# Two-layer decoder trunk: roots on ScalarE, relisted mixer steps, first loads issued together, last half stored in quarters

## The chip, the cores and the metric

The kernel runs on one core of a Trainium2 chip. The metric is the device time of one execution in microseconds (us); less is better. Engines are called as in the profile: PE is TensorE (PEld its weight loads), DVE is VectorE, ACT is ScalarE, POOL is GpSimd, SP is SyncE, which issues most of the DMAs.

## The reference

Two layers over x (256 tokens, 1024 features, float32), conditioned on a vector c. Cut to what matters:

```python
c_act = silu(c)
for l in range(2):
    sh1, sc1, gt1, sh2, sc2, gt2 = split(c_act @ w_ada[l] + b_ada[l], 6)
    h = rms_norm(x, g_pre_mix[l]) * (1 + sc1) + sh1
    q, k, v, pz = split(h @ w_in[l])              # 512 columns each
    ao = moba_attention(rotary(q), rotary(k), v)  # 8 heads, causal (one block of 256)
    po = multiscale_pool(pz, w_pool[l], pool_scale[l])
    y = concat(rms_norm(ao, a_gain[l]), rms_norm(po, p_gain[l])) @ w_out[l]
    x = x + gt1 * rms_norm(y, g_post_mix[l])
    h = rms_norm(x, g_pre_ffn[l]) * (1 + sc2) + sh2
    a, g = split(causal_conv3(h @ w_up[l]) + conv_b[l])   # 2816 columns each
    x = x + gt2 * rms_norm((silu(a) * g) @ w_down[l], g_post_ffn[l])
```

`rms_norm(x, g)` is `x / sqrt(mean(x*x) + 1e-6) * g`. Every norm thus needs a reciprocal root of one number per token.

## The kernel before

**Precision and parts.** Each float32 weight block is split on the chip into a high part (a cast on ScalarE, `Stream.high`, line 135) and a low part (a subtraction on VectorE, `Stream.low`, line 143), and each product is made as three matmuls (`mm3`, line 174). Activations are split in the same way. Weights thus pass through DMA, ScalarE and VectorE before TensorE can use them.

**Loads.** `Stream` (lines 77 to 159) holds one list of weight units in the order of use. `pump` (line 102) issues the next loads on SyncE's queue as long as one of 4 raw slots of 1 MB is free; a unit's slot is freed when its last part has been made or, for the modulation weights, when VectorE's reductions over them are done. Parts go into 8 high and 8 low buffers of 512 KB; in the FFN, parts are made up to `LEAD` = 6 ahead.

**Start** (lines 1000 to 1027, and `mixer`, line 475). c, x (two tiles of 128 tokens), the identity and the biases are loaded, all on SyncE's queue, then the first weight units. A matmul spreads c over the partitions, ScalarE applies Silu. VectorE squares and sums x, POOL takes the power -0.5, VectorE scales both tiles, TensorE transposes them (16 of 128 x 128), ScalarE copies the result in four pieces. Then the input projection of layer 0 runs over 8 chunks of 128 features: for each, `chunk(k)` (line 501) makes two reductions on VectorE (`dot`: modulation columns), the scale, two parts and the normalised activation; then 24 matmuls follow. The first modulation block and the first and last projection blocks are loaded as two half units, each of which takes a slot.

**Mixer steps** (`steps`, line 554). Everything between the input projection and the FFN is cut into some 250 small steps with two-letter names, and `ORDER[l]` (line 29) lists them by hand, one list per layer. While the list is worked off, the engines are "held" (`Kept`, line 59): each keeps its instructions in the order of the list, so an instruction that waits holds up all behind it on its engine. Names that matter here: `cq ck cv cz` copy the projections out of PSUM (a capital letter: on ScalarE instead of VectorE), `sc mx ex rc nm pt at` are the attention, `wo` the output projection, `gp gq` the gate products over a gate weight block, `gr gs gc gd gm gn` turn them into columns, `gt gg` make the gate row, `s2` reductions for the FFN's scale, `hi lo` make weight parts. The end of a list is a chain: `ss` (column sums of squares), `r1 r2` (roots of both group norms), `ad` (adds the two halves of y), `yq` (squares of y), `yG` (y times gate), `ry` (root), `xu` (x updated), `xs` (squares of x), `rx` (root), `xN` (x scaled), `tr` (transposes for the FFN). `tx` and `ts` load ScalarE's tables for Exp and for Silu by an activation of one dummy column (`table`, line 291).

**Roots.** `rstd` (line 386) takes two half sums, and on POOL adds epsilon, adds the second half, and raises to -0.5: three instructions. `r1 r2` (lines 774 to 784) use three instructions on VectorE and two on POOL.

**FFN** (`ffn`, line 885 on). For each of 22 column groups: up-projection, convolution (`conv_glu`: two scalings on ScalarE, four multiply-adds on VectorE, Silu on ScalarE between them), a split, down-projection. Six down-projections are kept for the end (`DEFER`), where `tail` (line 409) works on the four blocks of 128 tokens by 512 columns: matmuls, squares on ScalarE, product with the gate on VectorE; after both halves the root, the update of x, and either the norm for the next layer or the store. Outside the lists the compile-time scheduler is free to reorder.

## Time and profile before

| what | value |
|---|---|
| median of 3 runs | 610.45 us (610.43 to 611.44) |
| the profiled execution | 611.41 us |
| its span, first to last instruction | 609.6 us |
| TensorE busy / weight loads | 584.1 us (96%) / 504.0 us (83%) |
| VectorE / ScalarE / POOL busy | 490.4 (80%) / 376.7 (62%) / 29.8 us (5%) |
| mean granted clock of TensorE | 0.993 |
| DMA | 149.08 MB, mean 245 GB/s |

How to read it: the span is what the engines' records cover, the execution's time has a little more around it. TensorE is busy nearly all the time, so time can be won only where it stands or runs at less than its full rate. Nearly all instructions carry one line number, 69, because `Kept` records them there; they are told apart by tile names (`qk v pz`: input projection, `y yp`: output projection, `u d`: FFN, `T`: transposes, `hi lo`: weight parts, `hh hl`: activation parts, `sqs`: squares, `ra ry rx`: roots).

### The profile page before, as it was taken

The page shows a single profiled execution, that of the slowest core. Times are in us where ns is not written, and L with a number is a line of the kernel's source. Part 1 is how long each engine was busy: PE and PEld are TensorE (multiplying, and loading weights), DVE is VectorE, ACT ScalarE, POOL GpSimd, SP SyncE. Part 2 cuts the span into 40 slices and gives each one's busy share as a digit, 9 for nine tenths or more (in the row PEclk, how much of TensorE's full clock was granted, in tenths as well). Part 3 has the DMA queues.
Part 4 walks back from the last instruction along what each step waited for, and adds up shares of the span by engine and source line. Part 5 has one row for each costly group of instructions (what it writes and reads, how often), then busy time and mean ns, then how long its engine had stood idle before and what let it go on. Part 6 is the DMA issues. An engine that isn't in the chain of part 4 may idle for free.

```text
span 609.6 us, 9688 instructions
## 1 busy us (share of the span) xinstructions
PE 584.1 (96%) x3732; PEld 504.0 (83%) x3732; DVE 490.4 (80%) x865; ACT 376.7 (62%) x664; POOL 29.8 (5%) x62
## 2 busy tenths in 40 slices
PE   5999899699999999999999999979999999999995
PEld 3887567499999999999858876659999999999984
DVE  5998798789999998978559687688989787777753
ACT  4457786777656555557447688768765655656641
POOL 1000100400000000000010000140000000000001
PEclk9999999899999999999999999999999999999999
DMA  8999996667888867864339846765676566455001
GB/s 297 402 395 340 395 366 260 276 210 275 336 297 322 301 262 277 300 236 145 132 114 378 293 145 252 286 228 189 216 280 263 208 215 255 162 197 205 4 1 69
DMA packets 22768, 149.08 MB, mean 245 GB/s; under 512 B 2881, under 2 KB 3265, under 8 KB 6210
## 3 DMA queue, kind: packets, MB, share of 16 engines
q1 hardware_dynamic: 22722, 148.47, 66.0%
...
HBM read 147.41 MB, written 1.05 MB: 244 GB/s over the span
## 4 chain that ended last, share of the span: by engine, by line
PE 76%; DVE 10%; DMA 5%; ACT 4%; POOL 2%; issue 2%; POOLq 0%; DVEq 0%; SPq 0%; ACTq 0%
PE u L69 41%; PE d L69 20%; PE qk L69 3%; DVE lo L69 3%; PE y L69 2%; DVE raw L69 2%; DMA raw<-w_out_d 2%; PE pz L69 2%; PE v L69 2%; ACT hi L69 1%; DMA raw<-w_in_d 1%; DMA raw<-w_gt_d 1%; PE T L69 1%; POOL rx L69 1%; ACT sqs L69 1%
## 5 line engine op out<-in xcount | busy, mean ns | idle before, releaser
L69 DVE TENSOR_TENSOR lo<-raw,hi 128x1024 fp32r<-128x1024 f32 (+1 forms) x184 | 217.7, 1197 | 29.5 <-ACT hi L69 29.1
L69 ACT CAST hi<-raw 128x1024 fp32r<-128x1024 f32 (+1 forms) x184 | 185.8, 1030 | 58.1 <-DMA raw<-w_in_d 14.8
L69 PE MATMUL u<-hh,hi 128*128 128x256 f32 x704 | 182.2, 282 | 0.3 <-ACT h L69 0.2
L69 PE MATMUL u<-hh,lo 128*128 128x256 f32 x704 | 181.8, 281 | 0.0
L69 PE MATMUL u<-hl,hi 128*128 128x256 f32 x704 | 138.8, 282 | 0.5 <-DVE hl L69 0.5
L69 PEld LDWEIGHTS u<-hh,hi 128*128 128x128 f32 x704 | 132.5, 188 | 2.0 <-ACT hh L69 0.4
L69 PEld LDWEIGHTS u<-hh,lo 128*128 128x128 f32 x704 | 132.5, 188 | 1.4
L69 PEld LDWEIGHTS u<-hl,hi 128*128 128x128 f32 x704 | 107.1, 188 | 1.0 <-DVE hl L69 0.9
L69 DVE SCALAR_TENSOR_TENSOR cv<-u,vecs,cv 128x254 f32<-128x254 f32 (+1 forms) x176 | 83.1, 479 | 26.5 <-ACT cv L69 24.2
L69 ACT ACTIVATE cv<-u,vecs 128x256 f32<-128x256 f32 x88 | 48.7, 558 | 56.0 <-PE u L69 55.9
L69 DVE CUSTOM_DVE_ANT_0 raw<-raw,cbc,vecs 128x1024 f32<-128x1024 f32 x64 | 81.2, 1278 | 1.1 <-DMA raw<-w_g_d 0.9
L69 PE MATMUL d<-hi,sh 128*128 128x512 f32 x176 | 69.7, 396 | 0.0
L69 PE MATMUL d<-lo,sh 128*128 128x512 f32 x176 | 69.2, 393 | 0.0
L69 PE MATMUL d<-hi,sl 128*128 128x512 f32 x176 | 68.6, 394 | 0.0
L69 PEld LDWEIGHTS d<-hi,sl 128*128 128x128 f32 x176 | 33.0, 188 | 7.8 <-DVE sl L69 0.2
L69 PEld LDWEIGHTS d<-hi,sh 128*128 128x128 f32 x176 | 33.1, 188 | 6.6 <-ACT sh L69 0.3
L69 PEld LDWEIGHTS d<-lo,sh 128*128 128x128 f32 x176 | 33.2, 189 | 6.1
L69 ACT CAST sh<-cv 128x256 fp32r<-128x256 f32 x44 | 17.6, 404 | 33.3 <-DVE cv L69 33.3
L69 ACT ACTIVATE cv<-cv 128x256 f32<-128x256 f32 x44 | 18.4, 417 | 17.7 <-DVE cv L69 17.6
L69 ACT ACTIVATE sm<-sm,st 128x128 f32<-128x128 f32 (+1 forms) x52 | 22.0, 448 | 6.6 <-DVE st L69 6.5
L69 DVE TENSOR_TENSOR sl<-cv,sh 128x256 fp32r<-128x256 f32 x44 | 18.4, 421 | 9.1 <-ACT sh L69 9.1
L69 PE MATMUL qk<-hi,hh 128*128 128x512 f32 x64 | 23.0, 419 | 2.9 <-ACT hh L69 2.9
...
## 6 DMA issues: line engine op xcount, KB each, us to landing
...
```

Source lines behind the costliest of these rows:

```text
L69: r = op(*a, **k)
```

## The change

1. *Roots on ScalarE.* `rstd` becomes one addition on POOL (first half sum plus epsilon), one Sqrt on ScalarE with that as its bias and the second half sum as its input, one reciprocal on VectorE. In the lists `ry` and `rx` become three steps each (`ey sy ry`, `eX sx rx`). `r1 r2` become one Sqrt, a reciprocal and a product. `ts` now loads the table of Sqrt; the one of Silu is loaded in `ffn` after the norm, and that of Sqrt again behind its last Silu. The start's own root stays on POOL.
2. *Lists anew.* Both `ORDER` lists are written anew. `cK0` and `cZ1` move copies to ScalarE in layer 0, some `tQ` go back to VectorE; in layer 1 the gate steps (`gc gm gt gg`) move from the end of the list to before and among the attention's steps; in layer 0 they stay near the end.
3. *First loads at once, first chunk shared.* c, identity and biases are loaded on ScalarE's queue. The second modulation block and the second projection block are loaded, in halves, into part buffers (`home`) instead of raw slots, so that the first three blocks of each kind are issued without a wait. Blocks in halves now take one slot. The start up to chunk 1 is held in program order. The cast of the first part is shared by ScalarE and VectorE, the scaling of the second x tile moves to ScalarE, three of the four copies of x come after chunk 0, and TensorE makes 8 and then 12 transposes of the identity into a bank that is written later (`warm`).
4. *Last stores.* The last half of x is updated and stored in two quarters (of 256 columns).

The diff, cut to its core:

```diff
 ORDER = [
...
-    "ml3 ss ts gc r1 gm wo101 r2 wo201 gt0 ad10 gt1 gg0 ad11 wo210 gg1 ad00 wo310 ad01 wo300 yG10 hi8 wo301 "
-    "yG00 yq00 wo111 yG01 yq01 wo211 hi9 lo8 wo311 ry0 yq11 xu01 gq1 yq10 yG11 gq2 xs01 xu00 ry1 xs00 gq3 "
-    "xu11 xs11 xu10 rx0 lo9 xs10 gs xN00 xN01 gd rx1 tr00 xN10 gn tr01 xN11 tr10 hi10 tr11 hi11 lo10 lo11",
+    "sq3 wo200 sa3 ml3 ss gm r1 gt1 r2 wo201 gg1 ad00 gt0 ad01 gg0 wo300 ad10 wo301 yq00 yG00 ey0 wo210 yq01 "
+    "sy0 yG01 ry0 wo310 xu00 gq1 yq10 ey1 yG10 xs00 wo011 eX0 xu01 ad11 gq2 hi8 hi9 wo111 lo8 wo211 xs01 sx0 "
+    "wo311 lo9 yG11 yq11 gq3 sy1 rx0 ry1 xN00 gs xu11 gd xu10 tr00 hi10 gn lo10 xs10 eX1 xs11 sx1 xN01 rx1 "
+    "xN10 tr01 hi11 xN11 tr10 tr11 lo11",
...
-    "sa3 hi12 ss hi13 lo12 wo200 cy10 r1 cy11 wo001 wo101 lo13 r2 hi14 wo201 lo14 hi15 gc ad00 wo010 gm wo110 "
-    "ad11 gt1 wo300 ad01 gg1 ad10 wo301 yq00 wo210 lo15 yq01 gt0 gg0 wo111 ry0 wo211 yG00 xu00 wo311 yG01 "
-    "wo310 yq11 xu01 yq10 gq2 yG10 xs00 yG11 gq3 xs01 ry1 xu11 xs11 xu10 rx0 xN00 xs10 xN01 tr00 gs tr01 gd "
-    "rx1 xN10 xN11 gn tr10 tr11",
+    "sa2 ml2 sa3 hi12 yP12 hi13 lo12 yP13 hi14 lo13 hi15 ss r1 lo14 r2 wo200 cy10 cy11 wo201 lo15 wo010 ad01 "
+    "wo110 ad00 wo301 ad10 wo300 yq01 wo011 yq00 yG00 ey0 sy0 wo210 ad11 ry0 wo310 xu00 wo111 yq10 yG01 ey1 "
+    "wo211 xs00 xu01 eX0 wo311 yG10 yq11 yG11 gq2 sy1 ry1 xs01 sx0 gq3 xu10 xu11 rx0 xs10 eX1 xs11 xN00 xN01 "
+    "sx1 rx1 tr00 gs xN10 tr01 xN11 gd tr10 gn tr11",
 ]
...
+            elif home:
+                t = self.pool.tile([128, 1024], F32R, tag=home, name=home, bufs=PART_BUFS).bitcast(F32)
             elif len(self.slots) < RAW_BUFS or self.done[self.slots[-RAW_BUFS]]:
...
+            for a, b in loads or ():
+                self.nc.sync.dma_start(t[:, a:b], src[:, a:b])
...
-    def high(self):
+    def high(self, shared=False):
...
+        if shared:
+            self.dve.tensor_copy(hi[:, 512:1024], src[:, 512:1024])
+            self.act.copy(hi[:, 0:512], src[:, 0:512])
+        else:
+            self.act.copy(hi[:, :b - a], src)
...
+    def root(ms, t):
+        se.activation(t[:, 1:2], ms[:, 1:2], AF.Sqrt, bias=t[:, 0:1])
+
+    def rstd(ms, name, eps=1):
         t = small(2, name)
-        ge.tensor_scalar(t[:, 0:1], ms[:, 0:1], EPS, None, op0=OP.add)
-        ge.tensor_tensor(t[:, 0:1], t[:, 0:1], ms[:, 1:2], op=OP.add)
-        ge.tensor_tensor(t[:, 1:2], t[:, 0:1], powc[:, 0:1], op=OP.pow)
+        with_eps(ms, t, eps)
+        root(ms, t)
+        ve.reciprocal(t[:, 1:2], t[:, 1:2])
         return t[:, 1:2]
+
+    def with_eps(ms, t, eps=1):
+        ge.tensor_tensor(t[:, 0:1], ms[:, 0:1], powc[:, eps:eps + 1], op=OP.add)
...
+            if last:
+                cuts = [(0, 512), (512, 768), (768, 1024)]
             r = rstd(ms[b], "ry")
-            for hf in range(2):
-                ve.scalar_tensor_tensor(xt[b][:, halves[hf]], yg[b][:, halves[hf]], r,
-                                               xt[b][:, halves[hf]], op0=OP.mult, op1=OP.add)
+            for a, e in cuts:
+                ve.scalar_tensor_tensor(xt[b][:, a:e], yg[b][:, a:e], r, xt[b][:, a:e], op0=OP.mult, op1=OP.add)
...
-            chunk(0)
+            spread(0)
+            warm(12)
+            ada1(0, 0)
+            pre_coef(0, False, 0, 1)
+            st.high(True)
+            nh.make(0, x_of(0), True, between=st.low)
+            st.high()
+            st.low()
+            for i in (2, 1, 3):
+                spread(i)
+            chunk(1)
+            hold(False)
...
-            ve.tensor_scalar(t[:, 0:4], srcs["ss"][:, 0:4], 1.0 / 512.0, EPS, op0=OP.mult, op1=OP.add)
-            ve.reciprocal(t[:, 4:6], t[:, 0:2])
-            ve.tensor_mul(t[:, 2:4], t[:, 2:4], t[:, 4:6])
+            se.activation(t[:, 0:4], srcs["ss"][:, 0:4], AF.Sqrt, scale=1.0 / 512.0, bias=powc[:, 1:2])
...
-            ge.tensor_tensor(t[:, 4:8], t[:, 0:4], powc[:, 0:1].to_broadcast([128, 4]), op=OP.pow)
-            ge.tensor_scalar(t[:, 8:10], t[:, 4:6], 1.0 / 32.0, None, op0=OP.mult)
+            ve.reciprocal(t[:, 4:8], t[:, 0:4])
+            ve.tensor_mul(t[:, 6:8], t[:, 6:8], t[:, 0:2])
...
         def ts():
-            table(AF.Silu)
+            table(AF.Sqrt)
...
+        table(AF.Silu)
         for k in range(NK):
...
         st.ahead(PART_BUFS)
+        with tc.issue_after(silu):
+            table(AF.Sqrt)
...
-    nc.sync.dma_start(row, c)
+    nc.scalar.dma_start(row, c)
...
+    warm(8)
...
-        ve.tensor_scalar(xn[b], xt[b], t[:, 1:2], None, op0=OP.mult)
+    ve.tensor_scalar(xn[0], xt[0], r0[0][:, 1:2], None, op0=OP.mult)
+    se.activation(xn[1], xt[1], AF.Copy, scale=r0[1][:, 1:2])
```

`warm(n)` is n transposes of the identity into one PSUM bank; `spread(i)` is the copy of a quarter of transposed x; `x_of(k)` its slice for chunk k; `hold(on)` sets the engines' held state.

## Rows read from the trace of the kernel before

**Rows 1.** Engines' busy times over the span, the profile's first part.

```profile
PE 584.1 (96%) x3732; PEld 504.0 (83%) x3732; DVE 490.4 (80%) x865; ACT 376.7 (62%) x664; POOL 29.8 (5%) x62
```

**Rows 2.** Timeline of TensorE, input projection (start us, us, engine, line, operation, tiles; [idle before]).

```profile
14.05 2.08 PE L69 MATMUL qk<-hi,hh 128*128 128x512 f32 x4 [2.12 <-ACT hh L69]
...
22.26 1.10 PE L69 MATMUL qk<-lo,hh 128*128 128x512 f32 x4
...
60.15 0.40 PE L69 MATMUL pz<-hi,hl 128*128 128x512 f32 x1
```

**Rows 3.** Timeline of ScalarE, copies of transposed x.

```profile
10.05 2.50 ACT L69 COPY xT<-T 128x512 f32<-128x512 f32 x4 [3.38 <-PE T L69]
```

**Rows 4.** Timeline of VectorE, chunk 1's first reduction and chunk 7's last low part.

```profile
16.45 1.28 DVE L69 CUSTOM_DVE_ANT_0 raw<-raw,cbc,vecs 128x1024 f32<-128x1024 f32 x1
...
55.53 0.42 DVE L69 TENSOR_TENSOR hl<-h,hh 128x256 fp32r<-128x256 f32 x1
```

**Rows 5.** Busy times by stretch (PE, PEld, DVE, ACT, POOL, clock, DMA share, GB/s).

```profile
20.00:40.00 20.00, 20.00 (x88) 16.23 (x87) 18.47 (x28) 10.64 (x15) 0.00 (x0) 1.00 1.01 410
```

**Rows 6.** Timeline of the DMA queue on SyncE, first issue after the first four blocks.

```profile
10.26 0.33 SPq L110 DMA_DIRECT2D raw<-w_a_d  x1
```

**Rows 7.** Chain that ended last, landing of the first x.

```profile
1.14 3.42 DMA x<-x_d
```

**Rows 8.** Timelines of VectorE and TensorE, first mixer's waits for loads.

```profile
63.24 2.36 DVE L69 TENSOR_TENSOR lo<-raw,hi 128x1024 fp32r<-128x1024 f32 x2 [1.50 <-ACT hi L69]
...
69.06 2.36 DVE L69 TENSOR_TENSOR lo<-raw,hi 128x1024 fp32r<-128x1024 f32 x2 [2.08 <-ACT hi L69]
...
70.50 1.06 PE L69 MATMUL gacc<-raw,ctt 128*32 128x512 f32 x8 [1.48 <-DMA raw<-w_gt_d]
```

**Rows 9.** Timelines of ScalarE and TensorE, end of the first mixer.

```profile
111.10 0.20 ACT L69 ACTIVATION_READ_ACCUMULATOR sqs<-y,ra 128x1 f32 x1
...
115.99 0.66 PE L69 MATMUL gT<-ident,grow 128*128 128x128 f32 x4 [4.18 <-ACT grow L69]
116.78 3.50 PE L69 MATMUL T<-ident,xn 128*128 128x128 f32 x16
...
121.57 0.73 PE L69 MATMUL u<-hl,hi 128*128 128x256 f32 x4 [0.33 <-DVE hl L69]
```

**Rows 10.** Busy times by stretch, one microsecond in that end.

```profile
119.00:120.00 1.00, 1.00 (x6) 1.00 (x5) 1.00 (x2) 0.81 (x2) 0.00 (x0) 0.50 1.05 434
```

**Rows 11.** Timelines of ScalarE, TensorE and POOL, end of the second mixer.

```profile
406.39 0.19 ACT L69 ACTIVATION_READ_ACCUMULATOR sqs<-y,ra 128x1 f32 x1
...
410.64 1.94 PE L69 MATMUL T<-ident,xn 128*128 128x128 f32 x8 [3.18 <-DVE xn L69]
...
411.32 0.57 POOL L69 TENSOR_TENSOR rx<-rx,powc 128x1 f32<-128x1 f32 x1
...
416.50 0.74 PE L69 MATMUL u<-hl,hi 128*128 128x256 f32 x4 [0.20 <-DVE hl L69]
```

**Rows 12.** Timeline of VectorE and the profile's DMA part, end of the kernel.

```profile
604.18 0.69 DVE L69 TENSOR_TENSOR yg<-d,gate 128x512 f32<-128x512 f32 x1 [3.49 <-ACT sqs L69]
...
605.16 1.42 DVE L69 SCALAR_TENSOR_TENSOR x<-yg,ry,x 128x512 f32<-128x512 f32 x2 [0.29 <-POOL ry L69]
...
out_dram<-x SPq DMA_DIRECT2D x4, 256.0 KB, 2.0
```

**Rows 13.** Timelines of ScalarE and VectorE, table load, dummy and reciprocal.

```profile
99.53 1.28 ACT L69 ACT_TABLE_LOAD   x1
100.83 0.20 ACT L69 ACTIVATE dummy<-dummy 128x1 f32<-128x1 f32 x1
...
101.65 0.17 DVE L69 RECIPROCAL ra<-ra 128x2 f32<-128x2 f32 x1
```

**Rows 14.** Busy times by stretch, one microsecond between the layers.

```profile
309.00:310.00 1.00, 0.29 (x1) 0.29 (x2) 0.66 (x1) 0.66 (x3) 0.47 (x2) 1.00 0.00 0
```

**Rows 15.** Timeline of ScalarE, cast of the last activation.

```profile
590.75 0.41 ACT L69 CAST sh<-cv 128x256 fp32r<-128x256 f32 x1 [1.53 <-DVE cv L69]
```

150 lines of the change are left out of this document (87 added, 63 removed), and 28 rows, old and new, of the table ORDER.

## The prediction

> **What bounds the kernel now.** I read the busy shares first. TensorE is busy for 96% of the span [rows 1], so what can be won is the 25.5 us in which it stands, and the page's slices say that these lie at the start, in the two mixers' ends and at the very end. So I then went through those four places in order of time, with the timeline of each engine, to see who was late.
>
> *Start.* TensorE's four first products of the input projection take 2.08 us, four later ones 1.10, and the projection's last ends at 60.55 [rows 2]. One product alone shows as 0.40, so starts lie (1.10 - 0.40) / 3 = 0.233 apart, and the 192 products (8 chunks of 24) need 44.7 us: without a loss they would have had to begin at 15.8. ScalarE reaches the first weight cast only after four copies of transposed x [rows 3]. VectorE begins chunk 1's reductions at 16.45 and ends chunk 7 at 55.95, seven chunks at 5.64 [rows 4]; this is slightly slower than TensorE's 5.59 (24 x 0.233), so both matter. The loads can run at 410 GB/s [rows 5], but the DMA queue's next issue after the first four blocks comes at 10.26 [rows 6], when a slot is free. The first x lands 3.42 us after its issue [rows 7].
>
> *First mixer.* VectorE waits 1.50 and 2.08 us for casts whose blocks have not landed, TensorE 1.48 for a gate block [rows 8]. After that TensorE's list is nearly unbroken.
>
> *Ends of the mixers.* In layer 0 the last square sum is read at 111.30, yet TensorE stands 4.18 us, does the sixteen transposes in 3.50 and reaches the first low product of the next stage at 121.57 [rows 9]; the granted clock has fallen to 0.50 there [rows 10], the 1.2 GHz level, after TensorE had stood. In layer 1 the read ends at 406.58, TensorE stands 3.18 us, eight transposes take 1.94, the low product comes at 416.50, and between lie POOL's small instructions, of which the power alone is 0.57 [rows 11].
>
> *Inside the FFN halves* TensorE has no gap that this change touches.
>
> **The change part by part.**
>
> 1. **First loads and shared first chunk.** Removed from the way to chunk 1: three of the four copies of x, 3 x 0.6 (2.50 for four that overlap) [rows 3], which now come after the casts. The second normalised half moves from VectorE to ScalarE, and half of the first cast from ScalarE to VectorE. I walk it through: reductions of chunk 0 from about 8.2 to 10.6, cast and scaling on ScalarE to 11.7, low parts to 14.45, so chunk 1 begins 2.0 earlier than 16.45 [rows 4]. On TensorE, 8 + 12 transposes of the identity fill the wait. They cost at most 20 x 0.22 = 4.4 us (3.50 / 16 [rows 9]) in time in which nothing else was ready, and would cost up to 1.5 if they outlasted the cast. If they also end the slow start, products begin near 12.3 and end at 12.3 + 44.7 = 57.0: a gain of 3.5. If only VectorE's 2.0 comes through, 2.0. I take **-3.2**, nearer the first, because TensorE's sum is the longer one. Loads: 6 MB rather than 2 MB of weights are issued before anything waits. By 410 GB/s from 2.3 us on, chunk 2's blocks are there at about 18 and 20.6, which is ahead of its reductions at 20.1 and its cast. The c, identity and bias loads go to ScalarE's queue: three issues there, at no cost, since its first work waits for c anyway; without that cover they would cost the issues themselves, below 1.5 together.
>
> 2. **First mixer's middle.** Blocks come earlier because the last chunk takes one slot instead of two and the DMA engines had 6 MB in hand. The 1.50, 2.08 and 1.48 [rows 8] overlap on two engines. All of it gone would be 2.5 on TensorE's side; none if the new list stands elsewhere. **-1.5** (0 to -2.5).
>
> 3. **Roots.** Before, a root in the FFN tail cost 605.16 - 604.18 = 0.98 from the last read to the update [rows 12]. After: one ScalarE instruction at 0.20 (the smallest activation [rows 13]), a reciprocal at 0.17 [rows 13] and two hand-overs of 0.05 to 0.1, about 0.5. POOL's remaining addition depends on the first half's sum alone and can hide behind the second half's, except where that half comes at once. In layer 0's end three roots follow each other on POOL from 111.30; after, two of them, 0.5 each, lie on the chain. Against it, the new list puts the last output block 1.2 later. Net for that end: **-1.7** (0 to -3.5; the larger if TensorE keeps its clock and the 3.50 becomes about 1.9). In layer 1's end the gate rows' transposes leave the list's last part as well, and the chain from the last read to the low product, 9.9 us before [rows 11], shrinks by two roots and by VectorE's late gate products: **-3.3** (-1.5 to -4.5).
>
> 4. **FFN tails.** Between the layers TensorE's idle is small: it worked 0.29 of the microsecond at 309 [rows 14], and later waits were filled with gate products. **-0.3** (0 to -0.9). At the very end the reciprocal queues behind VectorE's gate product (604.18 + 0.69 = 604.87), so the update starts near 605.0: -0.15, not the 0.45 of the root.
>
> 5. **Table loads.** Four more: Silu after the norm of each FFN, Sqrt after its last Silu. Each 1.28, plus 0.20 for the dummy [rows 13]. The first of each pair lies before ScalarE's block of weight casts, with parts for six steps in hand: nothing; 1.5 if that cover were gone. The second falls into ScalarE's 1.53 us before the cast of the last activation [rows 15]: 1.48 fits. **+0.2** in all (0 to +3.0 if the load stands ahead of that cast's inputs, twice 1.48).
>
> The Trainium skill, "ScalarE: Activation LUTs", section "What ACT_TABLE_LOAD costs", gives a switch a drain of about 1.38 us besides the load. Our load shows no idle time before it and the next instruction runs at its end [rows 13], so this trace shows no drain. By the page's figure the two gaps would overflow by about 1.3 each, an estimate, and the sum would be near 602.4.
>
> 6. **Second mixer's middle.** Its waits on TensorE are few; I take **-0.4** (+1.0 to -0.8).
>
> 7. **Last stores.** 256 KB land 2.0 after issue [rows 12]. The updates of a half and two quarters take about the 1.42 of two halves plus 0.05; the last store is half as large: its bytes at 410 GB/s are 0.3 less. One more issue on the DMA queue fits beside the second update. **-0.3** (+0.1 to -0.6).
>
> Sum: -3.2 - 1.5 - 1.7 - 3.3 - 0.3 - 0.15 + 0.2 - 0.4 - 0.3 = **-10.65**. The profiled execution took 611.41 (span 609.6 and 1.8 around it), 0.96 above the median of the runs, so it would become 600.8, and the median 610.45 becomes **599.8**. Differences within 0.2% (1.2 us) I count as no change, about what a measurement of this kernel can tell.
>
> **Rivals.**
>
> *The lists stand elsewhere.* Both mixers' lists are fixed by hand on four engines; if an instruction is listed ahead of an input that arrives later than assumed, its whole engine stands. For it: the list of before made TensorE stand for a gate block [rows 8]. Against: the loads come earlier now. The two middles give nothing and the ends half: +1.9 + 2.5, so 604.2.
>
> *Table loads come through.* The Sqrt load is placed directly behind the last Silu and ahead of the second half's scaling, so that the cast of the last activation is 1.48 late, and TensorE with it, in both layers: +2.8, so 602.6. For it: TensorE came to that operand just as it was ready. Against: the gap of 1.53 [rows 15]. The page named above would make this case likelier, to which it adds the drain.
>
> *Slower: x lands late.* x now shares the DMA engines with eight weight blocks of 512 KB, where it had four, and two of 1 MB. If transfers share the rate evenly instead of landing in the order of issue, x's last byte waits until each of the transfers has moved about 0.5 MB: 12 x 0.5 MB at 410 GB/s is 15 us instead of 3.42 [rows 7], so the start is 11 late: +11 + 3.2 - 10.65, so 614. It decides when x lands later than about 13 us after its issue. Against: x came before the four blocks queued behind it.
>
> *Not done.* If the lists kept the POOL steps' old places or the compiler put further table loads between Square and Sqrt in the tails (1.28 each, some ten of them), the gains of the ends would be eaten: about 610. Against: Square, Copy and Identity ran beside Exp and Silu without a further load.
>
> **Numbers.** Forecast as summed, with the clock kept or not: 0.62. Lists: 0.19. Tables: 0.09. Late x: 0.06. Not done: 0.04. The likeliest gives 599.8. The unknowns of the ends and the start reach from 595 to 605, which takes in the lists' and the tables' cases: range 595.0 to 605.5. Faster by over 0.2%: 0.91; same 0.03; slower 0.06.
>
> **What would show it.** Right: the projection's last product ends near 57; the gap of TensorE in the ends is under 3 us, and no POOL power instruction lies in the tails; the nine table loads, none directly ahead of a cast that TensorE waits for; the low products at about 6 and 10 us earlier than before by layer. Wrong: x landing after 10; VectorE's chunk period above 5.65; a new TensorE wait above 1 us in either mixer.

## The result and the profile after

The changed kernel takes **608.12 us** (median of 6 runs, 606.24 to 608.59); the kernel before, on the same chip, 610.93 (610.43 to 611.58). The ratio is 0.9949, 95% interval 0.9930 to 0.9967: 0.5% faster, 2.8 us where 10.65 were forecast, and outside the range of 595.0 to 605.5. The profiled execution took 608.22 (span 606.4, 1.8 around it). The runs of the changed kernel lie in two groups, near 606.3 and near 608.3, with mean granted clocks of 0.994 to 0.997 and 0.989 to 0.992, and its median lies in the upper one.

TensorE is busy for 97% of the shorter span, 4.6 us longer than before [rows 1]:

*Busy time, share and instructions of each engine, after.*

```profile
PE 588.7 (97%) x3752; PEld 506.7 (84%) x3752; DVE 492.7 (81%) x884; ACT 383.5 (63%) x683; POOL 12.5 (2%) x31
```

Busy time at the low clock counts like any other, and so do the 20 identities, so this says little of the gain. I cut both spans into stages at the same instructions. The square sums' product is the small product `ss` that ends a mixer's middle. A low product is one with the low part of the activations, `hl`; the second group of them is the second `u<-hl` row of an FFN, from where TensorE's stream runs nearly without a gap again.

| stage, up to | before | after | change of the stage | forecast |
|---|---|---|---|---|
| projection's last product ends | 60.55 | 59.41 | -1.14 | -3.2 |
| layer 0: square sums' product | 100.39 | 99.19 | -0.06 | -1.5 |
| layer 0: second group of low products | 123.09 | 122.92 | +1.03 | -1.7 |
| first transposes for layer 1 | 308.36 | 307.89 | -0.30 | +0.1 |
| first product of layer 1's second half | 317.50 | 317.75 | +0.72 | -0.3 |
| layer 1: square sums' product | 394.15 | 394.52 | +0.12 | -0.4 |
| layer 1: second group of low products | 418.02 | 415.26 | -3.13 | -3.3 |
| last product ends | 603.36 | 600.60 | 0.00 | +0.1 |
| end of the span | 609.6 | 606.4 | -0.44 | -0.45 |

(The forecast's +0.2 for the tables is split over the two FFNs.) The last three rows came as forecast, with the tables in them. Nearly all that is missing lies in four places: the start (2.1), layer 0's middle (1.4), layer 0's end (2.7) and between the layers (1.0).

*Start, after: first and last products on TensorE, chunk 2's and 3's first reductions on VectorE, the cast that waited on ScalarE [rows 2 to 4].*

```profile
13.88 1.17 PE L70 MATMUL qk<-hi,hh 128*128 128x512 f32 x4
59.01 0.40 PE L70 MATMUL pz<-hi,hl 128*128 128x512 f32 x1
...
15.36 1.28 DVE L70 CUSTOM_DVE_ANT_0 hi<-hi,cbc,vecs 128x1024 f32<-128x1024 f32 x1
19.51 1.28 DVE L70 CUSTOM_DVE_ANT_0 raw<-raw,cbc,vecs 128x1024 f32<-128x1024 f32 x1 [0.45 <-DMA raw<-w_a_d]
26.70 1.28 DVE L70 CUSTOM_DVE_ANT_0 raw<-raw,cbc,vecs 128x1024 f32<-128x1024 f32 x1
...
22.01 1.06 ACT L70 CAST hi<-raw 128x1024 fp32r<-128x1024 f32 x1 [2.00 <-DMA raw<-w_in_d]
```

The first four products took 1.17, full rate at once. Still the projection's end moved by 1.14, no more than chunk 1's reductions did (16.45 to 15.36): VectorE's gain carries through, not TensorE's full rate. VectorE's wait of 0.45 for a block of chunk 2 (`w_a_d`) is new; ScalarE waited for the other one (`w_in_d`, 2.00 here) before the change too.

*Layer 0's end, after: timeline of all engines, and the window with the low clock, PEclk the third number from the end [rows 9, 10].*

```profile
111.97 0.19 ACT L70 ACTIVATION_READ_ACCUMULATOR sqs<-y,ra 128x1 f32 x1
112.20 0.29 ACT L70 ACTIVATE ry<-msy,ry 128x1 f32<-128x1 f32 x1
112.52 0.16 DVE L70 RECIPROCAL ry<-ry 128x1 f32<-128x1 f32 x1 [1.10 <-ACT ry L70]
113.02 0.66 PE L70 MATMUL gT<-ident,grow 128*128 128x128 f32 x4 [1.46 <-ACT grow L70]
116.27 2.82 PE L70 MATMUL T<-ident,xn 128*128 128x128 f32 x12 [2.16 <-DVE xn L70]
117.98 0.56 ACT L70 ACTIVATE hh<-T,mod,coef 128x256 fp32r<-128x256 f32 x1
122.92 0.64 PE L70 MATMUL u<-hl,hi 128*128 128x256 f32 x4
...
115.00:122.50 7.50, 6.23 (x30) 6.24 (x31) 7.43 (x14) 7.37 (x18) 0.63 (x1) 0.54 0.83 313
```

TensorE's wait of 4.18 became 1.46 and 2.16, and the last root is in its place, 0.29 on ScalarE and 0.16 for the reciprocal. But the last square sum is read at 111.97 where it was 111.10 [rows 9], although the stage began 1.2 earlier: 2.1 later in the stage. The chain from that read to the first hh shrank from 8.1 us (111.10 to 119.19) to 6.0 and only made that good. Then the granted clock stood at 0.50, the 1.2 GHz level, for 6.8 us, in which the transposes and the first products of the next stage ran at half rate; before it was 3.4 us.

*Between the layers: TensorE before, then after.*

```profile
313.69 0.39 PE L69 MATMUL v<-hi,hl 128*128 128x512 f32 x1
314.21 0.66 PE L69 MATMUL T<-ident,xn 128*128 128x128 f32 x4
314.79 2.78 PE L69 MATMUL gacc<-raw,ctt 128*32 128x512 f32 x22
```

```profile
310.77 1.90 PE L70 MATMUL gacc<-raw,ctt 128*32 128x512 f32 x10
...
313.17 0.39 PE L70 MATMUL v<-hi,hl 128*128 128x512 f32 x1
313.49 1.04 PE L70 MATMUL gacc<-raw,ctt 128*32 128x512 f32 x2
314.47 0.66 PE L70 MATMUL T<-ident,xn 128*128 128x128 f32 x4
315.05 2.77 PE L70 MATMUL gacc<-raw,ctt 128*32 128x512 f32 x20
317.75 0.50 PE L70 MATMUL qk<-hi,hh 128*128 128x512 f32 x1
```

The faster root won little here: TensorE waits 0.69 us for the first hh where it waited 0.75. And before, the transposes stood directly behind `v<-hi,hl`. Here two rows of a gate product are ahead of them, 1.04 us, although VectorE had finished the first half of xn at about 313.0 (it began both halves at 312.58 and took 0.88).

What that costs is seen in the starts of the gate products (`gacc`, only 32 columns wide, 32 of them in this stage). Up to four start within 0.02 us of each other, and the next ones 0.43 later, so that what counts is the number of such rounds. Before, the 32 made ten rounds; here they are cut into three pieces and make twelve. Two rounds more are 0.86 us, more than the 0.72 that the stage lost.

*Layer 1's end on TensorE, and the end of the span, after [rows 11, 12]; then ScalarE around the last of the nine table loads [rows 13, 15].*

```profile
413.74 0.74 PE L70 MATMUL u<-hl,hi 128*128 128x256 f32 x4 [0.33 <-DVE hl L70]
...
601.35 0.69 DVE L70 TENSOR_TENSOR yg<-d,gate 128x512 f32<-128x512 f32 x1 [3.51 <-ACT sqs L70]
601.96 0.15 DVE L70 RECIPROCAL ry<-ry 128x1 f32<-128x1 f32 x1
...
587.95 0.41 ACT L70 CAST sh<-cv 128x256 fp32r<-128x256 f32 x1 [1.53 <-DVE cv L70]
588.38 1.28 ACT L70 ACT_TABLE_LOAD   x1
589.67 0.20 ACT L70 ACTIVATE dummy<-dummy 128x1 f32<-128x1 f32 x1
```

The low product of layer 1 comes 2.8 earlier than [rows 11]. The end is as forecast: the reciprocal waits for the gate product. This load went behind the last cast, not into the wait before it, and TensorE did not wait for it.

### The profile page after: what moved, and what is told of

Its sections match the earlier page's. It is cut to its first block, busy times and chain, and to the rows that moved or that the text cites. A ratio compares the mean times of both kernels' runs of the same rounds, so it can differ in the third digit from the quotient of the medians.

```text
span 606.4 us, 9725 instructions
## 1 busy us (share of the span) xinstructions
PE 588.7 (97%) x3752; PEld 506.7 (84%) x3752; DVE 492.7 (81%) x884; ACT 383.5 (63%) x683; POOL 12.5 (2%) x31
## 4 chain that ended last, share of the span: by engine, by line
PE 89%; DVE 5%; ACT 3%; issue 1%; DMA 0%; DVEq 0%; ACTq 0%
PE u L70 41%; PE d L70 20%; PE qk L70 7%; PE v L70 3%; PE pz L70 3%; PE y L70 3%; PE yp L70 2%; DVE lo L70 2%; PE gacc L70 2%; PE T L70 1%; ACT sqs L70 1%; PE sc L70 1%; ACT sm L70 1%; DVE yg L70 1%; DVE x L70 1%
## 5 line engine op out<-in xcount | busy, mean ns | idle before, releaser
L70 ACT CAST hi<-raw 128x1024 fp32r<-128x1024 f32 (+1 forms) x182 | 183.4, 1025 | 61.4 <-PE u L70 15.7
L70 DVE CUSTOM_DVE_ANT_0 raw<-raw,cbc,vecs 128x1024 f32<-128x1024 f32 x62 | 78.8, 1281 | 1.6 <-DMA raw<-w_g_d 0.8
L70 ACT CAST sh<-cv 128x256 fp32r<-128x256 f32 x44 | 17.6, 404 | 33.3 <-DVE cv L70 33.3
L70 ACT ACTIVATE sm<-sm,st 128x128 f32<-128x128 f32 (+1 forms) x46 | 19.9, 462 | 6.9 <-DVE st L70 6.9
```

The source lines that it names most:

```text
L70: r = op(*a, **k)
```

## The experiments

Kernel n is the row en of the table. Each was compared with the kernel before as timed in the same session (medians 610.47 to 611.56). Stages of the profiled executions, in us; "low" is how long the granted clock stood at 0.50 in the two mixers' ends. The columns run from the projection's end to the square sums' product (middle 0), on to the second group of low products (end 0), from the first transposes for layer 1 to the first product of its second half (between), and from layer 1's square sums' product to the second group of low products of its FFN (end 1).

| kernel | us (range) | ratio to before | projection ends | middle 0 | end 0 | between | end 1 | low 0 / 1 |
|---|---|---|---|---|---|---|---|---|
| before | 610.93 | 1 | 60.55 | 39.84 | 22.70 | 9.14 | 23.87 | 3.4 / 3.4 |
| changed | 608.12 (606.24-608.59) | 0.9949 | 59.41 | 39.78 | 23.73 | 9.86 | 20.74 | 6.8 / 3.4 |
| e1_fill | 607.65 (607.08-608.36) | 0.9952 | 59.12 | 39.74 | 23.56 | 9.86 | 20.12 | 0 / 0 |
| e2_c_sync | 606.97 (606.59-607.35) | 0.9940 | 59.86 | 39.78 | 22.42 | 9.89 | 20.12 | 3.4 / 0 |
| e3_no_w12 | 607.15 (606.65-608.08) | 0.9945 | 59.54 | 39.78 | 22.49 | 9.88 | 20.12 | 3.4 / 0 |
| e4_no_warm | 606.60 (606.20-607.39) | 0.9936 | 58.76 | 39.74 | 23.05 | 9.89 | 21.34 | 3.4 / 3.4 |
| e5_old_lists | 607.41 (606.59-610.53) | 0.9949 | 59.05 | 37.74 | 21.15 | 9.88 | 23.27 | 3.4 / 3.4 |
| e6_no_wa1 | 605.83 (604.65-607.29) | 0.9916 | 57.56 | 39.73 | 23.09 | 9.87 | 21.26 | 3.4 / 3.4 |
| e7_swap | 606.06 (605.68-607.13) | 0.9922 | 59.41 | 39.75 | 22.53 | 9.88 | 20.13 | 3.4 / 0 |
| e8_pin | 605.30 (604.77-607.57) | 0.9915 | 59.58 | 39.78 | 23.55 | 9.88 | 20.18 | 6.8 / 3.4 |
| e9_mix | 605.70 (604.72-608.61) | 0.9912 | 59.04 | 38.71 | 21.14 | 9.88 | 21.60 | 3.4 / 3.4 |
| e10_pow | 607.25 (606.08-607.74) | 0.9932 | 58.81 | 39.78 | 23.47 | 9.00 | 20.48 | 3.4 / 0 |
| e11_trans | 604.60 (604.37-606.15) | 0.9895 | 58.77 | 39.74 | 23.01 | 7.93 | 20.38 | 3.4 / 3.4 |
| e12_all | 601.99 (601.49-603.90) | 0.9856 | 59.50 | 38.36 | 22.16 | 7.92 | 20.45 | 6.8 / 3.4 |
| e14_all_fill | 601.07 (600.94-601.68) | 0.9841 | 60.04 | 38.35 | 21.14 | 7.91 | 19.40 | 0 / 0 |
| e15_old_start | 608.71 (607.97-610.19) | 0.9969 | 61.50 | 39.77 | 22.61 | 9.85 | 20.14 | 3.4 / 0 |
| e16_fill_pow | 603.05 (601.84-603.83) | 0.9871 | 59.12 | 38.66 | 21.74 | 8.15 | 19.50 | 0 / 0 |

The intervals of the ratios are 0.0015 to 0.0026 to either side, 0.9 to 1.6 us. The stages are the sharper instrument in places: middle 0 is 39.73 to 39.78 in all eleven kernels of the table that have the new list of layer 0, and end 1 is 20.12 to 20.14 in the five kernels with the changed kernel's code there whose clock stayed up. Where the clock falls they are blunter: with the same list and the same 3.4 us of low clock, end 0 takes 22.42 to 23.09 and end 1 20.18 to 21.60. The low stretch does not fall on the same products each time (409.0 to 412.6 us in layer 1 of the changed kernel, 407.0 to 410.6 in kernel 4); that this makes the difference is not shown.

**1. The waits filled.**

```diff
-gq3 sy1 rx0 ry1 xN00 gs xu11 gd xu10 tr00 hi10
+gq3 wm1 sy1 rx0 ry1 xN00 gs xu11 gd xu10 tr00 wm2 hi10
...
-sx0 gq3 xu10 xu11
+sx0 gq3 wm2 xu10 xu11
```

> The changed kernel, with 24 more transposes of the identity in layer 0's mixer end (8 while TensorE waits for the gate row, 16 while it waits for the rest of xn) and 16 in layer 1's (while it waits for xn). Nothing else moves. Theory, the clock: in the changed kernel TensorE ran at 1.2 GHz from 115.8 to 122.4 in layer 0 and from 408.8 to 412.5 in layer 1, after it had stood, so the 1.2 us that the work ahead of it had won came down to 0.17 at the second group of low products. With the waits filled the clock should stay at 1.00, the twelve transposes of 2.82 take about 1.4, and the first FFN's second group of low products come from 122.92 to between 119.9 and 121.4; layer 1's end wins 0.5 to 1.5: in all 2.0 to 4.5 us less than the 608.1 of the changed kernel, 603.6 to 606.1. Rival, the other engines: VectorE's and ScalarE's chain to xn, hh and hl sets when the low products run, and the clock only fills time; then under 0.5 us. Rival, the fill is in the way: the transposes outlast the waits, and it is 0.5 or more slower.

607.65, ratio 0.9952 (0.9933 to 0.9970). The clock stood at 1.00 throughout, yet end 0 took 23.56. The experiment was not clean: ScalarE's order, which a program builds, now had three weight casts in a row ahead of the first hh.

*ScalarE of this kernel in layer 0's end.*

```profile
115.73 2.92 ACT L70 CAST hi<-raw 128x1024 fp32r<-128x1024 f32 x3
118.56 0.56 ACT L70 ACTIVATE hh<-T,mod,coef 128x256 fp32r<-128x256 f32 x1
```

So the time settles for the rival by its number, under 0.5 less, but not for its reason. In layer 1, where nothing else moved, end 1 fell from 20.74 to 20.12, the same as in executions whose clock stayed up by itself (kernels 2, 3 and 7).

**2. c on SyncE's queue.**

```diff
-    nc.scalar.dma_start(row, c)
+    nc.sync.dma_start(row, c)
```

> The changed kernel, with c loaded on the DMA queue of SyncE again, ahead of x; identity and biases stay on ScalarE's queue. Theory, the late c: cb starts at 2.3 rather than 3.33, the eight identity transposes end near 7.9 and not at 8.98, x's transposes start at 8.3 when xn is there rather than at 8.77, and the projection's last product ends 0.3 to 0.6 earlier than 59.45; the time falls by as much. x itself is issued 0.35 later and may land that much later, which takes up to 0.35 back. Rival: the start is set further down the chain (identity transposes that run until 13.88 although the operands of the first product are there at 12.75), so the first product stays at 13.9 and the time does not move (within 0.3).

606.97 (0.9922 to 0.9958). c's product began at 2.25, but so it did with c on ScalarE's queue (2.23 to 2.50 in the first, third and fourth kernels); the 3.33 of the changed kernel's profile was that execution's own. First product 14.07, projection's end 59.86: the rival.

**3 and 4. Without the identity transposes at the start** (third kernel: the twelve; fourth: all twenty).

```diff
-            warm(12)
...
-    warm(8)
```

> The changed kernel without the twelve identity transposes that stand between x's transposes and the first product; the eight ahead of x's stay. Theory, they outlast the operands: hh is ready at 12.75, the twelve run to 13.9; without them the first product starts near 12.8, and if the clock rises as early as it does now (near 13.0) the projection ends 0.8 to 1.1 earlier, at 58.4 to 58.7. Rival, they buy the clock: without them TensorE stands from 12.39 to 12.8, the first products run at half rate (four in 2.08, as before the change) and nothing is won, or up to 1.0 is lost: the projection's end at 59.4 to 60.5.

> The changed kernel with none of the twenty identity transposes. x's transposes then start when xn is there, at 8.3 rather than 8.77, and hh comes 0.5 earlier, near 12.25. Theory, the identities cost as much as they win: the first product starts near 12.3, runs at half rate until about 16, loses some 1.5 against full rate, and the projection ends within 0.4 of the 59.45 of the changed kernel. Rival, only the clock matters at the start: the end of the projection is 1 us or more later than 59.45. Rival, the clock rises by itself as TensorE is busy from 8.3 on: the end is 1 us or more earlier.

The first product came at 11.97 and 11.59, about two microseconds earlier than 13.88, and the projection ended at 59.54 and 58.76 (the first kernel, with all twenty and c landing early: 12.41 and 59.12). By the projection's end kernel 3 is in its rival's range, but not for the rival's reason: its four first products took 1.20, full rate. Kernel 4 lies between its theory and its second rival. So here the identities are worth nothing that shows, and neither is TensorE's earlier start: something behind it takes it back. They are not without effect everywhere: in kernels 12 and 16, which have none, the four first products took 2.08, as before the change, and the projection ended at 59.50 and 59.12.

*Fourth kernel, VectorE: the first reductions of chunks 1 to 3.*

```profile
14.15 1.28 DVE L70 CUSTOM_DVE_ANT_0 hi<-hi,cbc,vecs 128x1024 f32<-128x1024 f32 x1
19.27 1.28 DVE L70 CUSTOM_DVE_ANT_0 raw<-raw,cbc,vecs 128x1024 f32<-128x1024 f32 x1 [1.42 <-DMA raw<-w_a_d]
26.46 1.28 DVE L70 CUSTOM_DVE_ANT_0 raw<-raw,cbc,vecs 128x1024 f32<-128x1024 f32 x1
```

Chunk 1 began 1.21 earlier than in the changed kernel, chunk 3 only 0.24: chunk 2 waits for its blocks.

**6. 1 MB less to load.** Chunk 1's modulation weights are set to zero by POOL.

```diff
+                if home == "hi":
+                    self.nc.gpsimd.memset(t[:, a:b], 0.0)
+                else:
                     self.nc.sync.dma_start(t[:, a:b], src[:, a:b])
```

> The changed kernel without the load of chunk 1's modulation weights (1 MB, the second pair of loads after the first four blocks): POOL sets these two tiles to zero instead, so the modulation of that chunk is its bias alone; every instruction on the values stays. Theory, the loads hold the start: chunk 2's blocks landed near 19.4 and 21.9 in all runs, however early chunk 1's reductions began (14.15 to 15.36), so with 1 MB less ahead of them they land 2 to 2.7 us earlier, chunk 3's reductions begin two chunk periods (11.3) after chunk 1's, at 25.4 to 25.7 where chunk 1 begins at 14.1 to 14.4, and the projection ends 0.7 to 1.3 earlier than 59.1. Rival, VectorE's pace alone: no DMA wait counts, chunk 3 begins 12.3 after chunk 1 as in the other runs and the projection's end stays at 58.8 to 59.5.

*VectorE in this kernel: one reduction of chunk 1, the first of chunk 3; then a window of the changed kernel's start (GB/s is the last number).*

```profile
14.60 1.28 DVE L70 CUSTOM_DVE_ANT_0 hi<-hi,cbc,vecs 128x1024 f32<-128x1024 f32 x1
24.79 1.27 DVE L70 CUSTOM_DVE_ANT_0 raw<-raw,cbc,vecs 128x1024 f32<-128x1024 f32 x1
...
2.00:6.00 4.00, 2.67 (x3) 1.16 (x4) 1.36 (x3) 1.87 (x2) 0.12 (x1) 1.00 0.97 353
```

Chunk 3 begins 10.2 after chunk 1, not 12.3, and the projection ends at 57.56, 1.2 to 2.5 earlier than in the kernels with the new start and the load. The loads hold the new start, by a little more than I had expected. They moved 353 GB/s from 2 to 6 us and 351 from 6 to 10, not the 410 of a later stretch. With the load away VectorE's last part is ready 5.5 us before the projection's end, in the changed kernel 4.5: then it is TensorE's own sum that counts.

**5 and 9. The old lists** with the new pieces of the roots in the places of the POOL roots: in both layers, then in layer 0 alone.

```diff
-    "wo311 lo9 yG11 yq11 gq3 sy1 rx0 ry1 xN00 gs xu11 gd xu10 tr00 hi10 gn lo10 xs10 eX1 xs11 sx1 xN01 rx1 "
...
+    "yG00 yq00 wo111 yG01 yq01 wo211 hi9 lo8 wo311 ey0 sy0 ry0 yq11 xu01 gq1 yq10 yG11 gq2 xs01 xu00 ey1 sy1 ry1 xs00 gq3 "
...
```

> The changed kernel with both mixers' lists of before, in which each root of before stands as its three new pieces (addition, ScalarE root, reciprocal) in the place where the POOL root stood. So the start, the roots, the tails and the tables are those of the change, and only the new lists are undone. Theory, in layer 0 the new list gives nothing: from the square sums' product to the second group of the FFN's low products the changed kernel needs 23.7 us (22.4 in other runs of the same code there), before 22.7; with the old list and the new roots it should be 20.7 to 21.7, because the last square sum is read 2 us earlier behind the square sums' product; but the middle of the first mixer should lose 0 to 1.5 again (waits for gate blocks). In layer 1 the new list matters: the second mixer's end loses 0.5 to 1.5 against the changed kernel. In all 606.5 to 609. Rival, the new lists are the gain and the roots none: then 609.5 to 611, near the kernel before less the 1.5 of the start.

> The changed kernel with layer 0's list of before (the new pieces of the roots in the places of the POOL roots, as in the run with both old lists) and layer 1's new list. Theory, each list where it stood better: in the run with both old lists the square sums' product came at 96.8 and the second group of low products at 117.9 (changed kernel 99.2 and 122.9), while the second mixer's end, from the last square sums' product to the second group of low products, took 23.3 there and 20.7 with the new list. Both together: 2 to 3.5 us less than the changed kernel, 604.0 to 606.3, of which the first FFN gives back 1.2 as it did there. Rival, the loads: the first FFN and the second mixer's lists then run ahead of their blocks and give back more than half; 606.5 to 608.

*TensorE in layer 0: square sums' product and second group of low products in the kernel before, in the changed kernel (second group above), in the fifth and in the ninth; then middle 0 of the first three by windows, TensorE's busy time first.*

```profile
100.39 0.35 PE L69 MATMUL ss<-ones,ssq 128*128 128x1 f32 x2
123.09 0.64 PE L69 MATMUL u<-hl,hi 128*128 128x256 f32 x4
...
99.19 0.28 PE L70 MATMUL ss<-ones,ssq 128*128 128x1 f32 x2
...
96.79 0.35 PE L69 MATMUL ss<-ones,ssq 128*128 128x1 f32 x2
117.94 0.64 PE L69 MATMUL u<-hl,hi 128*128 128x256 f32 x4
...
97.75 0.35 PE L69 MATMUL ss<-ones,ssq 128*128 128x1 f32 x2
118.89 0.64 PE L69 MATMUL u<-hl,hi 128*128 128x256 f32 x4
...
60.55:100.39 39.84, 37.22 (x237) 24.74 (x238) 34.17 (x99) 32.97 (x83) 2.21 (x3) 1.00 0.97 370
59.41:99.19 39.78, 38.88 (x241) 25.19 (x241) 35.56 (x100) 33.35 (x84) 3.22 (x3) 1.00 0.91 334
59.05:96.79 37.74, 36.91 (x237) 24.78 (x238) 34.04 (x99) 32.80 (x83) 2.22 (x3) 1.00 0.95 368
```

This is the main finding. With the new start and new roots but **layer 0's old list**, middle 0 takes 37.74 and 38.71 (before 39.84) and end 0 21.15 and 21.14 (before 22.70, at the same 3.4 us of low clock): together -3.7 and -2.7 against before, where the forecast had -3.2. With the new list they take 39.7 to 39.8 and 22.4 to 23.7: it gives all of that back.

The windows show how in the middle. Under the new list TensorE no longer stands, 0.9 us instead of 2.6, but it is busy for 1.7 us longer at the same clock of 1.00. Part of that is four transposes of a gate row (`gT`), which the new list does ahead of the square sums and the old one behind them: 0.4 from the first of them to the next instruction. Most of the rest are the 24 attention transposes (`pT`), the same in both: counted from each start to the next instruction's start they take 2.3 us before and in the fifth kernel and 4.1 in the changed one, 0.7 of it standing. That is where the time goes; which step of the list would have to move back was not tested. It also sets right what I wrote on the profile of before, that time can be won only where TensorE stands or runs below its full rate: here 1.7 us lie in products that run at the full clock, and 1.9 between the layers (kernel 11).

In layer 1 the new list is the gain: end 1 is 23.27 with the old list and 20.18 to 21.60 with the new one at the same 3.4 us of low clock.

The whole program shows less than the stages, because with layer 0's old list the first FFN takes 186.6 us from its second group of low products to the next transposes, 1.6 more than in the changed kernel and 1.3 more than before: TensorE waits 0.2 there for hl and 0.7 for the cast of the last activation. Counted with the FFN, from the projection's end to the first transposes for layer 1, the kernel before takes 247.8, the kernels with layer 0's new list 247.2 to 248.5, and those with the old one 246.4 and 245.4 (kernels 9 and 5). The forecast for these three rows was -3.1; with the old list -1.4 and -2.4 came, with the new one -0.6 to +0.7. By the median the mixed kernel, 605.70, is inside the forecast of its theory, but its interval, 0.9886 to 0.9938, overlaps the changed kernel's: the stages carry this finding, not the time. With both old lists it is 607.41, as expected.

**7. Square ahead of the gate product** in layer 0's list.

```diff
-lo9 yG11 yq11 gq3 sy1
+lo9 yq11 yG11 gq3 sy1
```

> The changed kernel with one exchange in layer 0's list: the square of the last output block (ScalarE) is listed ahead of its gate product (VectorE), not behind it. Both read the same block of PSUM; in the changed kernel the square began only when the product was done, 111.39 after 110.60. Theory, the gate product stands on the way: the last square sum is read 0.6 to 0.8 earlier, xn with it, and the second group of low products comes 0.4 to 0.8 earlier behind the square sums' product than in the changed kernel (22.4 to 23.7, by how long the clock is low). Rival, it only changes places: the product now waits for the square, and the update of x behind both comes no earlier; 0.2 or less.

The square began at 110.54 and xn was there 0.39 earlier, but end 0 took 22.53, as in two kernels without the exchange and with the same low clock (22.42, 22.49): the rival in the stage. The time, 606.06 (0.9902 to 0.9942), overlaps the changed kernel's interval. Not settled by more than the stage.

**8. ScalarE held to the written order** while hh and h are made.

```diff
+        se.held = True
         for k in range(NK):
             nh.make(k, nh.src(k), True)
             ...
+        se.held = False
```

> The changed kernel with ScalarE held to the written order while the FFN's first operands are made. In the changed kernel ScalarE ran the cast of a weight block that is needed much later ahead of the first hh of layer 0 (two casts in a row, 1.98, from 116.09), so hh came at 117.98. Theory, the cast is in the way: hh comes 0.3 to 0.9 earlier behind xn and TensorE's first product with it, and the second group of low products 0.3 to 0.9 earlier in layer 0; layer 1, where it stood behind, stays. Rival, TensorE at the low clock is late anyway (its transposes end near 117.6 to 118): under 0.3. Rival, the cast is late where it is needed: a new wait of TensorE of 0.5 or more in the first steps of the FFN.

The profiled execution took 607.57, the median is 605.30 (0.9893 to 0.9938). Its profile shows hh at 118.00 with 0.72 of waiting for TensorE's transposes, which ran at the low clock: no gain in end 0 (23.55), the first rival's case. A gain shows in layer 1, which the theory said would stay: end 1 is 20.18 against 20.74, with the same low stretch, and TensorE's low products come 0.4 earlier in the program. With layer 0's old list the hold shows in the FFN: the first FFN, from its second group of low products to its last product, takes 185.4 in the twelfth kernel and 186.7 in the ninth, and the waits for hl and for the cast are gone.

**10. Roots back on POOL** in the changed kernel.

```diff
-        se.activation(t[:, 1:2], ms[:, 1:2], AF.Sqrt, bias=t[:, 0:1])
+        ge.tensor_tensor(t[:, 0:1], t[:, 0:1], ms[:, 1:2], op=OP.add)
+        ge.tensor_tensor(t[:, 1:2], t[:, 0:1], powc[:, 0:1], op=OP.pow)
```

> The changed kernel with its roots on POOL again: in the place of each ScalarE root stand an addition and a power on POOL, and the reciprocals are gone; lists, table loads, start and tails are those of the change. It prices the roots alone. Theory, a root on POOL costs 0.4 to 0.6 more on the chain, and two of them lie on the chain of each mixer's end: second groups of low products 0.6 to 1.2 later behind the last square sum in each layer, 0.3 at the very end where the reciprocal queued behind the gate product, so 1.5 to 2.7 slower than the changed kernel: 609 to 610.8 by the runs of it (606.2 to 608.6). Rival, the lists alone made the ends shorter: within 0.5 of the changed kernel.

607.25 (0.9913 to 0.9952), 0.9 less than the changed kernel and not more: nearer to the rival. Two things hide the root: this execution had 6.8 us less of low clock, and between the layers it took 9.00, because there the transposes stood directly behind the low products again and the gate products made ten rounds, as before. So the loss between the layers came with the faster roots: the order that is built there put gate products first, and I take the other time of xn for the reason.

**11. TensorE's order written out between the layers.**

```diff
+            te.held = True
...
+                    gap(0, 2)
+                    for o, w, c0 in outs:
+                        te.matmul(o, hl, w[0][:, c0:c0 + 512], start=False, stop=False, skip_group_check=True)
...
+            gap(2, 4)
+            te.held = False
```

> The changed kernel with TensorE's order written out between the layers: the six first products, two gate blocks, the three low products, the second four transposes, two gate blocks. In the changed kernel two gate products stood between the low products and the transposes, 1.04 long, although xn was there at 313.02, and from the first transposes to the first product of the second half it took 9.86 us against 9.14 before. Theory, that order costs it: 8.6 to 9.3 here, 0.5 to 1.2 us less, and it stays in the end. Rival, TensorE has the same work in any order: 9.5 to 10, no change.

7.93 instead of 9.86, and 604.60 (0.9875 to 0.9914): more than expected, and it stays. The rival, that TensorE has the same work in any order, is out, though the reason was not the one that I had: the 32 gate products now make two pieces of four full rounds, and sixteen of them take 1.92, as long as ten took in the changed kernel. Four rounds fewer are 1.7 of the 1.93 us.

*TensorE between the layers, this kernel.*

```profile
312.04 0.60 PE L70 MATMUL T<-ident,xn 128*128 128x128 f32 x4
312.56 1.92 PE L70 MATMUL gacc<-raw,ctt 128*32 128x512 f32 x16
314.42 0.50 PE L70 MATMUL qk<-hi,hh 128*128 128x512 f32 x1
```

**12. What won, together**: edits 4, 8, 9 and 11.

> What won in the single runs together: layer 0's old list and layer 1's new one, no identity transposes at the start, ScalarE held to the written order while the FFN's operands are made, TensorE's order written out between the layers. Theory, the gains are on one chain and add: 2.5 from the list (less the first FFN's 1.2), 0.5 to 0.8 from the cast (605.3 with that alone), 0.5 to 1.0 between the layers, 0 to 0.7 at the start: 602.0 to 604.5. Rival, the later stages are set by their loads, so that what comes earlier waits there: 604.5 to 606.5.

601.99 (0.9833 to 0.9880), at the lower end of the theory's range. The gains add only in part: by the medians the four edits alone are 10.3 below the changed kernel in sum, together 6.1, and the interval still touches that of edit 11 alone.

**13 and 14. The waits filled again**: as in 1 with edit 8, and in the twelfth kernel (24 identities ahead of the gate rows' transposes in layer 0, 16 in layer 1).

```diff
-xs00 gq3 xu11
+xs00 gq3 wm3 xu11
```

> The changed kernel with the waits of both mixers' ends filled by 24 and 16 transposes of the identity, and ScalarE held to the written order while the FFN's operands are made, so that no cast is moved ahead of them as it was in the first run with the fill. Theory, the clock: 605.3 with the order held alone; with the clock at 1.00 the second group of low products comes 0.8 to 2 us earlier behind the square sums' product in layer 0 (23.6 there, with 6.8 us at the low clock) and 0.3 to 1 in layer 1: 602.5 to 604.5, and the runs lie closer together. Rival, VectorE's and ScalarE's chain sets the end: 604.8 to 605.8.

> The kernel with all that won (601.99) and the waits of the mixers' ends filled: 24 transposes of the identity in layer 0 before the gate rows' transposes, 16 in layer 1 before those of xn. Theory, the clock: its profiled run had 6.8 us at the low clock in layer 0's end and 3.4 in layer 1's, of which half is lost where TensorE is the one that is waited for: 599.5 to 601.3. Rival, the other engines are waited for: 601.5 to 602.5.

The thirteenth took 605.67 (605.45 to 606.88; ratio 0.9918, 0.9896 to 0.9940): nothing against edit 8 alone, so the rival. Its profiled execution has a granted clock of 0.95 from about 9 us on, unlike all others, and I don't compare its stages. The fourteenth took **601.07** (0.9818 to 0.9865), the fastest kernel here, and its runs lie within 0.8 us. That is what the theory of the clock said, and end 0 and end 1 are each 1.0 shorter than in the twelfth. But the intervals of the two overlap, and the thirteenth points the other way: what the fill is worth over the whole program is not settled.

*Twelfth, then fourteenth kernel: layer 0's end by windows, PEclk as above.*

```profile
105.00:120.00 15.00, 11.67 (x71) 9.02 (x70) 12.23 (x24) 13.43 (x34) 2.56 (x4) 0.77 0.75 287
```

```profile
105.00:120.00 15.00, 13.62 (x101) 9.72 (x100) 12.74 (x25) 14.01 (x34) 2.58 (x4) 1.00 0.70 282
```

**15. The old start in the changed kernel** (the start's code of before in place of the new).

```diff
-    nc.scalar.dma_start(row, c)
+    nc.sync.dma_start(row, c)
...
-            spread(0)
-            warm(12)
+            chunk(0)
...
```

> The changed kernel with the start of before: the loads in the old order and on SyncE's queue, transposed x copied in four steps ahead of chunk 0, no shared cast, no identity transposes, chunk 7's loads in halves. It prices the first part alone. Theory: the projection ends at 60.3 to 60.8, 1.1 to 1.8 later than in the runs with the new start, and the time is 0.8 to 1.8 above the 606.2 to 608.6 of the changed kernel. Rival, the new start's loads pay later, in the first mixer (blocks there earlier): 2 to 3.5 above. Rival, the start is worth nothing in the end, because the first FFN waits for its loads anyway: within 0.5.

608.71 (0.9954 to 0.9984). The projection ended at 61.50, later than in the kernel before with the same start; the first products began at 14.02, as there, but ran at half rate until 19.3 instead of 17.6. By the ratios the start is worth 0.0020 of 611, 1.2 us, by the medians 0.6, and the intervals overlap. Middle 0 is 39.77 with either start as long as the new list stands: it pays nothing later there.

**16. Roots on POOL with the clock held**: edit 10 in the fourteenth kernel.

> The kernel with all that won and filled waits, with the roots on POOL again (an addition and a power in the place of each ScalarE root, no reciprocals). It prices the roots where the clock is held. Theory, the root is 0.4 to 0.5 shorter on ScalarE (0.84 from the last read to xn in the changed kernel, 1.28 with POOL), twice in each mixer's end and once in each tail: 1.2 to 2.5 slower than the filled kernel with ScalarE roots. Rival, what else the engines have to do at these places hides it: 0 to 0.6 slower.

603.05 (0.9848 to 0.9893), 1.98 slower: the theory, with no run of one kernel among those of the other, though the intervals overlap. By stages: end 0 +0.60, between +0.24, end 1 +0.10, the very end +0.23 (6.07 from the last product against 5.84), 1.2 in all where roots stand. Another 0.7 lies in the middles and 0.3 in the first FFN, where no root of this edit stands, and the projection ended 0.9 earlier. So a root on POOL costs 1.2 us by the stages that hold one and 2.0 by the medians. The POOL root of before has one instruction more than this one, so the pair does not price all that the change did to the roots.

*The last read to xn in layer 1: fourteenth, then sixteenth kernel.*

```profile
403.43 0.18 ACT L69 ACTIVATION_READ_ACCUMULATOR sqs<-x 128x1 f32 x1
403.70 0.29 ACT L69 ACTIVATE rx<-msx,rx 128x1 f32<-128x1 f32 x1
404.03 0.16 DVE L69 RECIPROCAL rx<-rx 128x1 f32<-128x1 f32 x1 [0.19 <-ACT rx L69]
404.23 0.88 DVE L69 TENSOR_SCALAR xn<-x,rx 128x512 f32<-128x512 f32 x2
```

```profile
404.30 0.18 ACT L69 ACTIVATION_READ_ACCUMULATOR sqs<-x 128x1 f32 x1
404.89 0.55 POOL L69 TENSOR_TENSOR rx<-rx,powc 128x1 f32<-128x1 f32 x1
405.48 0.88 DVE L69 TENSOR_SCALAR xn<-x,rx 128x512 f32<-128x512 f32 x2 [1.02 <-POOL rx L69]
```

0.80 against 1.18 from the start of the read to xn, so a root is 0.38 shorter on ScalarE. Counted from the read's end, as my working counts, it is 0.62 against 1.00: I had 0.5 against 0.98, a saving of 0.48.

## Why the prediction was wrong

Most of the miss comes from two steps, the path chosen for the start and layer 0's new list.

1. **Start: -3.2 taken, -1.1 measured.** The step that failed is "nearer the first, because TensorE's sum is the longer one". TensorE's sum gave no bound: the first products came up to 2.3 earlier in other runs and the projection's end did not follow. The other path, VectorE's, came to its 2.0 where c landed early (chunk 1 began 2.2 and 2.3 earlier in kernels 1 and 4) and to 1.1 in the profiled execution, where c landed late. Where chunk 1 comes earlier still, a wait for chunk 2's blocks takes it back (1.42 in kernel 4). I had put these blocks at 18 and 20.6 by 410 GB/s; they landed near 19.3 and 22. The sixth kernel shows the loads, kernels 3 and 4 that TensorE's start is not it. The identities did outlast the operands, as the bound of 1.5 allowed (hh was there at 12.75, the twelve ran to 13.9), and it cost nothing that shows.
2. **First mixer's middle: -1.5 taken, -0.06 measured.** The waits did vanish: 2.6 us of TensorE's standing became 0.9. With the old list that paid 1.1 to 2.1 (kernels 5, 9, 12 and 14). The new list spends it, not by waits but in products that take longer where they stand now. The step that failed is to take the new list as neutral where no wait was named.
3. **Roots.** In layer 0's end -1.7 was taken and +1.0 measured. The step that failed is "the new list puts the last output block 1.2 later": the last read came 2.1 later in its stage. With the old list the stage gets 1.55 shorter, close to the term, but not by the roots alone: about half of it, 0.74, lies between the last read and xn, where the roots stand (111.10 to 116.15 before, 107.30 to 111.61 in kernel 5), 0.2 ahead of that and 0.6 behind it, and the first FFN then gives 1.3 back. On top of it the low clock lasted 3.4 longer in the profiled execution. In layer 1's end -3.3 was taken and -3.13 measured. My working had both causes there, the list and two roots, but not their shares: 1.7 to 3.1 of it is the list (23.27 with the old one, 20.18 to 21.60 with the new one at the same 3.4 us of low clock), and the roots give 0.60 under the old list (23.87 to 23.27) and 0.10 between kernels 14 and 16. That the number came out so near is in part luck. A root was mis-sized too: it costs 0.62 from the read's end to its use, not 0.5, because the ScalarE instruction is 0.29 and not the 0.20 of the dummy. The Trainium skill, "ScalarE: Activation LUTs", section "What ACT_TABLE_LOAD costs", gives about 0.28 us for an activation of one element with a bias from memory; the 0.29 agrees, and the dummy has no such bias.
4. **FFN tails.** The very end came as worked out. Between the layers -0.3 was taken and +0.72 measured: I costed the root and not the order behind it. That order changed with the roots (kernel 10), and it cut the gate products into twelve rounds where there were ten; eight are enough (kernel 11).
5. **Table loads.** Right: nine loads, none seen by TensorE. The drain that this section of the Trainium skill gives did not show: in the rows above the load follows the cast at once and the dummy follows the load.
6. **Second mixer's middle**: +0.12, inside its bounds.
7. **Last stores**: together with the update -0.44, against -0.45.

Of the rivals, "the lists stand elsewhere" came true in its place, layer 0, and its direction, but not by its mechanism: TensorE stood less (0.9 for 2.6 us in the middle, 3.6 for 4.2 in the end), its products took longer and the last read came later. Its price of 4.4 was too low, since it took the lists to give nothing in the middles and half in the ends, while layer 0's list took the ends whole and more. Late x did not happen: x's first reduction began at 4.49. Of the signs, the nine tables and the tails without a POOL power came as stated; the projection's end at 57, the low products 6 us earlier in layer 0 (0.2 came) and 10 earlier in layer 1 (2.8 came) did not.
